# A decoder layer on one core: a larger share of the first down part in units of seven products, with two weight sums made by an accumulating DMA

## The chip, the cores and the metric

The kernel runs on one core of one Trainium2 chip. The metric is the device time of one execution in microseconds. Five engines have instruction queues of their own that run in order: TensorE (PE; its weight loads are shown as PEld), VectorE (DVE), ScalarE (ACT), GpSimd (POOL) and SyncE (SP). SP issues most loads, POOL some; they wait for one another through semaphores.

## The reference

One layer of a hybrid decoder, 256 tokens, width 2048, all in float32. What matters here is its last third:

```python
def conv_ffn(h, w_up, conv_w, conv_b, w_down):
    a, b = jnp.split(h @ w_up, 2, axis=-1)
    ...
    return (jax.nn.gelu(c, approximate=True) * b) @ w_down

    h = rms_norm(x, norm_ffn_pre[l])
    y = conv_ffn(h, ffn_w_up[l], ffn_conv_w[l], ffn_conv_b[l], ffn_w_down[l])
    x = x + rms_norm(y, norm_ffn_post[l])
```

`w_up` is 2048 x 11264, `w_down` 5632 x 2048. `c` is a causal convolution of width 3 over `a`. Before it come the mixer's parts: one projection `w_in` (with two gate blocks), two attentions, their output projections `wo_a` and `wo_b`, and `w_out`.

## The kernel before

Each float32 operand is split into a high part, rounded for TensorE, and the low part that is left. A product of a 128-row block is three matmuls: high x high, high x low, low x high (`mm3`, lines 174 to 177; a moving tile has 512 columns). `convert` splits a loaded weight tile: ScalarE casts the high part (L143), VectorE subtracts it (L144). Split tiles live in a ring of five, plain rows arrive through `raw` tiles loaded by SP.

Tokens go in two blocks of 128. A pair of 128-row weight blocks (k = 2u and 2u + 1) times two token blocks and two column halves of 512 is eight products, so 24 matmuls: a plain unit (`plain`). In a unit of seven (`seven`) the same is done as in Strassen's scheme by seven products, 21 matmuls, from sums of the four weight quarters (`ta`, `tb`, on VectorE, L232 to L235) and sums of the four token quarters (`s_of(u)`, made earlier by `token_sums`). Its products go to four accumulators `c` and four accumulators `q`; at the end of a part the `q` are added into `d` in a fixed order, and `c` on top of that.

`pair_gemm` runs a string of units, "p" plain and "s" seven. It is used for the gate part (one pair of column blocks of `w_in`, "psppspsp") and for the first down part: the first 24 of 44 row blocks of `w_down`, in two halves of 1024 columns (tiles `cd0`/`qd0`, `cd1`/`qd1`), twelve units each:

```python
PAIR_ORDER = ("psppsppsppsp", "ppsppsppsppp")
```

The two rows of a unit of seven are loaded by POOL, whole (1024 columns): `even` and `odd`, into a tile of tag `gp` (one buffer, for the odd-numbered sevens: `rr1`, `rr3`, ...) or into two tiles of tags `fa` and `fb` (two buffers each: `rr2a`, `rr2b`, ...). The `f` tags are shared with the up part's outputs `f0_5`, `f1_5`.

Most of the kernel is not written in its final order: a scheduler places each engine's instructions after their program order and the free buffers. Work that need not be done at once is put in by steps: `at(t, f)` keeps f for the t-th tick, `tick()` runs what is due.

Of the kernel before, what the change touches and what calls it, by code (L numbers as in the profile page):

```python
# [41 lines left out]
def trunk_layer(ctx, tc, x, x_cols_in, conv_cols_in, g_mix_post, g_ffn_post, w_in, w_q, w_kv,  # L42
                sinks, rel, wo_a, wo_b, w_out, w_up, w_down, rope_tab, strip_sel, out):
    nc = tc.nc
    vec, act, pe, pool = nc.vector, nc.scalar, nc.tensor, nc.gpsimd
# [13 lines left out]
    def sb(pl, shape, name, dt=F32, tag=None, bufs=None):  # L59
        return pl.tile(shape, dt, name=name, tag=tag or name, **({"bufs": bufs} if bufs else {}))  # L60
# [41 lines left out]
    cnt = [0]  # L102
# [52 lines left out]
    now = [0]  # L155

    def at(t, *fs):
        steps[max(t, now[0])].extend(fs)

    def tick():  # L160
        for f in steps.pop(now[0], ()):
            f()
        now[0] += 1

    def drain():
        while steps:
            tick()
# [33 lines left out]
    def banks(kind, name):  # L201
        return [(pacc if kind == 0 else (pss, pst)[i // 2]).tile([P, 512], F32, name=f"{name}{i}", tag="acc" if kind == 0 else "st"[i // 2])
                for i in range(4)]

    def pair_gemm(name, w, k0, c0, order, act_of, s_of, kind, d, place, sums):

        c11, c12, c21, c22 = c = banks(kind, f"c{name}_")
        q, used = [], set()
        row = lambda k: w[(k0 + k) * P:(k0 + k + 1) * P, c0:c0 + 1024]
        half = lambda w_, i: tuple(x[:, i * 512:(i + 1) * 512] for x in w_)  # L210

        def mul(o, x, w_, last=False):
            mm3(o, *x, *w_, id(o) not in used, last)
            used.add(id(o))

        def plain(u, last):
            for k in (2 * u, 2 * u + 1):
                w_ = convert(raw_row(row(k)), 1024)
                for t in range(NT):
                    for j in range(2):  # L220
                        mul(c[2 * t + j], act_of(k, t), half(w_, j), last and k % 2 == 1)
                tick()

        def seven(u, last):
            s1, s2, s3, s4 = s_of(u)
            even, odd = place()
            pool.dma_start(even, row(2 * u))
            pool.dma_start(odd, row(2 * u + 1))
# [4 lines left out]
            vec.tensor_tensor(ta[:, hi_], odd[:, hi_], even[:, hi_], op=ALU.subtract)  # L233
# [12 lines left out]
            tick()  # L246
            w_ = convert(tb, 1024)
            mul(q6, s2, half(w_, 0), last)
            mul(c21, act_of(2 * u + 1, 1), half(w_, 1))
            tick()  # L250
            if last:
                act.copy(d[0], q1)
                vec.tensor_tensor(d[1], d[0], q6, op=ALU.add)
                vec.tensor_tensor(d[2], d[1], q7, op=ALU.add)
                vec.tensor_tensor(d[3], d[2], q5, op=ALU.add)
                vec.tensor_tensor(d[1], d[1], q5, op=ALU.add)
# [11 lines left out]
    def token_sums(g, a, m, hi, lo):  # L268
# [4 lines left out]
        vec.tensor_tensor(m1, a21, a22, op=ALU.add)  # L273
        vec.tensor_tensor(m3, a11, a21, op=ALU.subtract)
        vec.tensor_tensor(m2, m1, a11, op=ALU.subtract)
# [82 lines left out]
    rh = sb(base, [P, NT], "rh")  # L358
# [297 lines left out]
    acc, _ = gemm(XH, XL, w_in, 0, KT, 0, 512)  # L656
# [4 lines left out]
    acc, _ = gemm(XH, XL, w_in, 0, KT, C_KV, KVR + ROPE)  # L661
# [54 lines left out]
    def gate_pair(j):  # L716
        d = [stg(f"tb{j + i}_{t}") for t in range(NT) for i in range(2)]
        c = pair_gemm("g", w_in, 0, C_GB + 512 * j, GATE_ORDER, lambda k, t: (XH(k)[:, t * P:(t + 1) * P], XL(k)[:, t * P:(t + 1) * P]),
                      lambda u: xs[u], 0, d, g_place, lambda: [sb(pg, [P, 1024], f"gt{n}{cnt[0]}", tag="gt" + n, bufs=2) for n in "ab"])
        for i, (o, x_) in enumerate(zip(d, c)):  # L720
            t = i // 2
            vec.tensor_tensor(o, o, x_, op=ALU.add)
            act.activation(o, o, AF.Tanh, scale=rh[:, t:t + 1])
        return [d[0], d[2]], [d[1], d[3]]

    tb = {0: gate_b(0)}
# [174 lines left out]
    es3, p3 = open_pool("p3")  # L901
# [5 lines left out]
    es6, p6 = open_pool("p6")  # L907
# [96 lines left out]
    for b in range(4):  # L1004
        c0, n = W_BLOCKS[b]
        last = b == 3
# [103 lines left out]
    gtiles, s_pool, s_of = [], [], {}  # L1110
# [10 lines left out]
    s_tiles = []  # L1121

    def g_sums(u):

        if u % 2 == 0:
            s_tiles.append(sb(p3, [P, D], f"s_{u // 2}", F32R, tag=f"x2_{u // 2}"))
        hi, lo = (s_tiles[u // 2][:, (u % 2) * 1024 + i * 512:(u % 2) * 1024 + (i + 1) * 512] for i in range(2))
        a, m = (sb(s_pool[0], [P, 512], f"s{n}{u}", tag="hx", bufs=2) for n in "am")
        s_of[u] = token_sums(gtiles[u].bitcast(F32), a, m, hi, lo)

    def gemm_cols(acc, c0):

# [40 lines left out]
    for c in range(1, 6):  # L1173
        if c == 2:
            for i in range(8):
                at(now[0] + i, lambda i=i: park(i // 4, i % 4))
        if c == 4:
            for u in range(4):
                at(now[0] + 3 + 3 * u, lambda u=u: g_sums(u))
        ffn_up(c, 4 * c)  # L1180

# [7 lines left out]
    def down_place():  # L1189
        sevens_done[0] += 1  # L1190
        i = sevens_done[0]
        if i % 2:
            both = sb(p6, [P, D], f"rr{i}", tag="gp")
            return both[:, 0:1024], both[:, 1024:2048]
        return [sb(p6, [P, 1024], f"rr{i}{n}", tag="f" + n, bufs=2) for n in "ab"]

    def f_sums():
        return [sb(p6, [P, 1024], f"t{n}{cnt[0]}", tag="f" + n, bufs=2) for n in "ab"]

    for p in range(2):  # L1200
        d = [dsum[t][2 * p + j] for t in range(NT) for j in range(2)]
        c = pair_gemm(f"d{p}", w_down, 0, 1024 * p, PAIR_ORDER[p], lambda k, t: (GH(k)[:, t * P:(t + 1) * P], GL(k)[:, t * P:(t + 1) * P]),
                      lambda u: s_of[u], p, d, down_place, f_sums)
        for o, x_ in zip(d, c):
            vec.tensor_tensor(o, o, x_, op=ALU.add)
# [44 lines left out]
    for j in range(4):  # L1250
        last = j == 3
# [103 lines left out]
```

## Time and profile before

| | |
|---|---|
| median of three runs | 1470.02 us (1469.75 to 1470.31) |
| profiled execution | 1469.86 us |
| its span, first to last instruction | 1468.0 us |
| TensorE busy | 1457.9 us, 7585 matmuls in the records |
| VectorE, ScalarE, GpSimd busy | 1044.5, 824.1, 61.7 us |
| first down part | 1002.35 to about 1128.3 us |

The page's idle time is what an engine spends without an instruction; only that of the engine on the chain costs time. A row of a group reads: line, engine, operation, output and inputs, shape, count, then busy time and mean. A POOL row of a DMA shows how long the issue took; the landing is told apart.

### The profile page before, as it was taken

To read this page: it belongs to the slowest core of one execution; us is meant where nothing else is said; L and a number is where in the kernel's file an instruction comes from. 1 tells how busy PE (TensorE), PEld (TensorE's weight loads), DVE (VectorE), ACT (ScalarE), POOL (GpSimd) and SP (SyncE) were. 2 spreads that over 40 slices of the span, in tenths; PEclk is the share of its full clock that TensorE was granted. 3 is DMA by queue.
4 is the path that set the end of the run, shared out by engine and by line. 5 is a ranking of instruction groups with operands and counts; after the bars stand their busy time and mean duration, and the time that the engine had idled before them with its cause. 6 is when DMAs were issued, how large, how long until landed. Compare 5 with 4: busy or idle time off the path is not lost.

```text
span 1468.0 us, 20901 instructions
## 1 busy us (share of the span) xinstructions
PE 1457.9 (99%) x7585; PEld 1246.1 (85%) x7585; DVE 1044.5 (71%) x1837; ACT 824.1 (56%) x1362; POOL 61.7 (4%) x107
## 2 busy tenths in 40 slices
PE   9999999999999999999999999999999999999997
PEld 7888888888888888888888888888888888888886
DVE  7788896646667665655699877678776676677556
ACT  7588874544565554444566655555454555555443
POOL 0022110000000010000000000000000000000000
PEclk9999999999999999999999999999999999999999
DMA  8755376466655559656665665655657656655653
GB/s 293 220 173 165 95 272 195 157 208 200 187 160 156 172 165 334 226 182 211 225 204 182 193 192 182 196 187 191 215 178 259 206 183 192 188 186 188 199 188 127
DMA packets 152467, 287.60 MB, mean 196 GB/s; under 512 B 18427, under 2 KB 29596, under 8 KB 152236
## 3 DMA queue, kind: packets, MB, share of 16 engines
q1 hardware_dynamic: 144736, 259.95, 55.2%
q0 software_dynamic: 7536, 26.27, 5.6%
q8 instruction: 59, 0.97, 0.3%
q14 instruction: 44, 0.36, 0.1%
q10 hardware_dynamic: 92, 0.05, 0.0%
HBM read 277.79 MB, written 8.44 MB: 195 GB/s over the span
## 4 chain that ended last, share of the span: by engine, by line
PE 97%; DVE 2%; ACT 1%; issue 0%; DMA 0%; DVEq 0%; ACTq 0%
PE accg L175 14%; PE accg L177 14%; PE accg L176 14%; PE ub L1138 10%; PE ua L1138 10%; PE ub L1142 5%; PE ua L1142 5%; PE cd L177 2%; PE cd L176 2%; PE cd L175 2%; PE mpo L866 1%; PE cg L175 1%; PE cg L177 1%; PE cg L176 1%; PE ms L832 1%; PE pt L521 1%
## 5 line engine op out<-in xcount | busy, mean ns | idle before, releaser
L144 DVE TENSOR_TENSOR wlo<-raw,whi 128x1024 fp32r<-128x1024 f32 (+2 forms) x482 | 583.8, 1215 | 313.2 <-ACT whi L143 306.5
L143 ACT CAST whi<-raw 128x1024 fp32r<-128x1024 f32 (+2 forms) x482 | 501.1, 1043 | 445.1 <-PE accg L177 212.8
L175 PE MATMUL accg<-whi,ahl 128*128 128x512 f32 (+1 forms) x480 | 187.9, 391 | 0.0
L177 PE MATMUL accg<-whi,ahl 128*128 128x512 f32 (+1 forms) x480 | 185.6, 387 | 0.0
L176 PE MATMUL accg<-wlo,ahl 128*128 128x512 f32 (+1 forms) x480 | 184.8, 385 | 0.0
L175 PE MATMUL accg<-whi,bhl 128*128 128x512 f32 x442 | 173.1, 392 | 0.0
L177 PE MATMUL accg<-whi,bhl 128*128 128x512 f32 x442 | 172.3, 390 | 0.0
L176 PE MATMUL accg<-wlo,bhl 128*128 128x512 f32 x442 | 172.2, 390 | 0.0
L1138 PE MATMUL ua<-ahl,whi 128*128 128x512 f32 x640 | 154.6, 391 | 0.0
L1138 PE MATMUL ub<-ahl,whi 128*128 128x512 f32 x640 | 154.6, 391 | 0.0
L1138 PEld LDWEIGHTS ub<-ahl,whi 128*128 128x128 f32 x640 | 117.5, 188 | 22.8 <-ACT cc L1036 0.2
L1138 PEld LDWEIGHTS ua<-ahl,whi 128*128 128x128 f32 x640 | 117.5, 188 | 22.7
L177 PEld LDWEIGHTS accg<-whi,ahl 128*128 128x128 f32 x480 | 90.1, 188 | 18.0
L176 PEld LDWEIGHTS accg<-wlo,ahl 128*128 128x128 f32 x480 | 90.3, 188 | 15.5
L175 PEld LDWEIGHTS accg<-whi,ahl 128*128 128x128 f32 x480 | 90.3, 188 | 15.4
L177 PEld LDWEIGHTS accg<-whi,bhl 128*128 128x128 f32 x442 | 83.0, 188 | 17.3
L176 PEld LDWEIGHTS accg<-wlo,bhl 128*128 128x128 f32 x442 | 83.0, 188 | 16.9
L175 PEld LDWEIGHTS accg<-whi,bhl 128*128 128x128 f32 x442 | 83.0, 188 | 16.9
L1142 PEld LDWEIGHTS ub<-ahl,wlo 128*128 128x128 f32 x640 | 82.2, 191 | 3.2
L1142 PEld LDWEIGHTS ua<-ahl,wlo 128*128 128x128 f32 x640 | 82.2, 191 | 3.1
L1142 PE MATMUL ua<-ahl,wlo 128*128 128x256 f32 x640 | 83.7, 283 | 0.0
L1142 PE MATMUL ub<-ahl,wlo 128*128 128x256 f32 x640 | 83.2, 283 | 0.0
(493 smaller groups left out, 2060.1 us busy)
## 6 DMA issues: line engine op xcount, KB each, us to landing
raw<-in_ffn_w_up_dram SPq DMA_DIRECT2D x176, 512.0 KB, 4.4
raw<-in_w_in_dram SPq DMA_DIRECT2D x105, 512.0 KB, 4.5
raw<-in_ffn_w_down_dram SPq DMA_DIRECT2D x74, 512.0 KB, 3.8
raw<-in_w_o_swa_dram SPq DMA_DIRECT2D x32, 512.0 KB, 4.3
raw<-in_w_o_mla_dram SPq DMA_DIRECT2D x32, 512.0 KB, 4.4
raw<-in_w_out_dram SPq DMA_DIRECT2D x32, 512.0 KB, 4.0
bias<-strip POOLq DMA_DIRECT2D x16, 256.0 KB, 4.3
raw<-in_mla_w_q_up_dram SPq DMA_DIRECT2D x32, 128.0 KB, 2.5
```

What stands on the lines that cost most here:

```text
L143: act.copy(hi[:, a:b], raw[:, a:b])
L144: vec.tensor_tensor(lo[:, a:b], raw[:, a:b], hi[:, a:b].bitcast(F32), op=ALU.subtract)
L175: pe.matmul(o, ah, bh, start=start, stop=False)
L176: pe.matmul(o, ah, bl, start=False, stop=False)
L177: pe.matmul(o, al, bh, start=False, stop=stop)
L521: pe.transpose(pt[:, j * P:(j + 1) * P], p[:, c * P:(c + 1) * P], ident)
L832: pe.matmul(o, w, v_, start=n == 0, stop=False)
L866: pe.matmul(o, w(t), p_[:, c], start=n == 0, stop=n == 5)
L1138: pe.matmul(acc[i], hi[:, c], hn[p][:, j * 512:(j + 1) * 512], start=p + j == 0, stop=stop)
L1142: pe.matmul(acc[i][:, 0:256], lo[:, c], hn[p][:, j * 512:j * 512 + 256], start=False, stop=False)
```

## The change

A second kind of unit of seven, `seven_dma`, is used in the first down part. POOL loads the even row into `x_`, the odd row into `odd`, the even row's left half once more into `even`, and then, with an accumulating DMA, adds the right halves of both rows onto `x_`. So `x_` holds even-left + even-right and even-right + odd-right, two of the four weight sums, with no instruction of VectorE; the other two (`y_`) are two additions. The signs of the token sums (`plus=True`) and of the closing sums are turned to match. The accumulating DMA waits on POOL's queue until the first load of `x_` has landed. The strings of units become "pspspspsppsp" and "ppspspspspsp": ten sevens in place of seven. The token sums of a fifth unit (`g_sums(4)`) are made in the up part, in a `gp` tile and two `hx` tiles. The closing sums of all pair parts, the gate part's too, are put in by steps (`first_sums`, `more_sums`, `finish_gate`) in place of at once, and the `drain()` after the gate part is gone.

```diff
+        def seven_dma(u, last):
+            s1, s2, s3, s4 = s_of(u)
+            x_, odd, y_, even = place()
+            lo_, hi_ = slice(0, 512), slice(512, 1024)
+            two = w[(k0 + 2 * u) * P:(k0 + 2 * u + 2) * P, c0 + 512:c0 + 1024].rearrange("(a p) n -> p a n", p=P)
+            pool.dma_start(x_, row(2 * u))
+            pool.dma_start(odd, row(2 * u + 1))
+            pool.dma_start(even[:, lo_], row(2 * u)[:, lo_])
+            pool.dma_start(x_.rearrange("p (a n) -> p a n", a=2), two, accum_op=ALU.add)
+            w_ = convert(odd, 1024)
...
+            mul(c11, act_of(2 * u + 1, 0), half(w_, 0))
+            mul(c12, s4, half(w_, 1))
+            w_ = convert(even, 512)
+            mul(q1, act_of(2 * u, 0), half(w_, 0), last)
+            w_ = convert(x_, 1024)
+            vec.tensor_tensor(y_[:, lo_], x_[:, lo_], odd[:, hi_], op=ALU.add)
+            vec.tensor_tensor(y_[:, hi_], y_[:, lo_], odd[:, lo_], op=ALU.add)
+            mul(q5, s1, half(w_, 0), last)
+            mul(q7, s3, half(w_, 1), last)
+            tick()
+            w_ = convert(y_, 1024)
+            mul(q6, s2, half(w_, 0), last)
+            mul(c21, act_of(2 * u + 1, 1), half(w_, 1))
+            tick()
...
+                at(now[0], first_sums)
+                at(now[0] + 1, more_sums)
...
-                seven(u, u == n - 1)
+                (seven if sums else seven_dma)(u, u == n - 1)
...
+        if plus:
+            vec.tensor_tensor(m1, a22, a21, op=ALU.subtract)
+        else:
+            vec.tensor_tensor(m1, a21, a22, op=ALU.add)
...
+        for n_, i in enumerate((0, 2, 1, 3)):
+            at(now[0] + n_, lambda i=i: finish_gate(i))
...
-    drain()
...
+        if u == 4:
+            t4 = sb(p6, [P, D], "s_tmp", tag="gp")
+            a, m = t4[:, 0:512], t4[:, 512:1024]
+            hi, lo = (sb(s_pool[0], [P, 512], f"s4{n}", F32R, tag="hx", bufs=2) for n in "hl")
...
+        f = lambda n: [sb(p6, [P, 1024], f"{n}{x_}{i}", tag="f" + x_, bufs=2) for x_ in "ab"]
         if i % 2:
             both = sb(p6, [P, D], f"rr{i}", tag="gp")
-            return both[:, 0:1024], both[:, 1024:2048]
+            x_, odd = both[:, 0:1024], both[:, 1024:2048]
+        else:
+            x_, odd = f("rr")
+        return x_, odd, *f("ty")
...
-PAIR_ORDER = ("psppsppsppsp", "ppsppsppsppp")
+PAIR_ORDER = ("pspspspsppsp", "ppspspspspsp")
```

The order of the instructions of POOL in the first half, before: the rows of the first four sevens (`rr1` to `rr4`; L227 loads an even row, L228 an odd one), with the storing of the residual between them.

```order
L227 DMA rr1_10019<-in_ffn_w_down_dram 128x1024
L228 DMA rr1_10019<-in_ffn_w_down_dram 128x1024
L1113 DMA x2_d_2541<-x2_1_5852 128x512 x4
L227 DMA rr2a_10180<-in_ffn_w_down_dram 128x1024
L227 DMA rr3_10299<-in_ffn_w_down_dram 128x1024
L228 DMA rr3_10299<-in_ffn_w_down_dram 128x1024
L228 DMA rr2b_10181<-in_ffn_w_down_dram 128x1024
L227 DMA rr4a_10417<-in_ffn_w_down_dram 128x1024
L228 DMA rr4b_10418<-in_ffn_w_down_dram 128x1024
```

In the changed kernel the same place, from the first seven on, reads as follows; L232 is the accumulating load (128x2x512), L231 the half tile `even` (`tyb`), L229 and L230 are x and odd.

```order
L229 DMA rra2_10141<-in_ffn_w_down_dram 128x1024
L232 DMA rra2_10141<-in_ffn_w_down_dram 128x2x512
L231 DMA tyb1_10031<-in_ffn_w_down_dram 128x512
L230 DMA rrb2_10142<-in_ffn_w_down_dram 128x1024
L229 DMA rr3_10237<-in_ffn_w_down_dram 128x1024
L230 DMA rr3_10237<-in_ffn_w_down_dram 128x1024
L232 DMA rr3_10237<-in_ffn_w_down_dram 128x2x512
L231 DMA tyb2_10144<-in_ffn_w_down_dram 128x512
L231 DMA tyb3_10239<-in_ffn_w_down_dram 128x512
L230 DMA rrb4_10320<-in_ffn_w_down_dram 128x1024
L231 DMA tyb4_10322<-in_ffn_w_down_dram 128x512
L229 DMA rra4_10319<-in_ffn_w_down_dram 128x1024
```

Each seven has four entries, and `tyb1` stands behind the accumulating load of the second seven, `tyb2` behind that of the third. `tyb2` takes the buffer of `rrb2`, the odd row of the same unit, and waits for the last reader of that; `rrb4` and `tyb4` take those of `tyb2` and `tyb3`, and wait until these are split. `rra4`, the fourth unit's x, stands behind `tyb4`.

On VectorE, before, around the first sums of the second seven (`ta682`, `tb682` from `rr2a`, `rr2b`; `wlo` is the low part of a split, `raw` a plain row):

```order
L232 TENSOR_TENSOR ta682_10184<-rr2a_10180 128x512
L1041 TENSOR_TENSOR uu23_10168<-uu23_10168,cc23_10167 128x256
L310 TENSOR_TENSOR ghl10_7551<-uu21_10070,ghl10_7551 128x256
L144 TENSOR_TENSOR wlo675_10085<-raw674_10082,whi675_10084 128x1024
L144 TENSOR_TENSOR wlo677_10103<-raw676_10100,whi677_10102 128x1024
L310 TENSOR_TENSOR ghl11_7552<-uu22_10119,ghl11_7552 128x256
L144 TENSOR_TENSOR wlo679_10134<-raw678_10131,whi679_10133 128x1024
L1043 SCALAR_TENSOR_TENSOR uu23_10168<-uu23_10168,cc23_10167 128x256
L233 TENSOR_TENSOR ta682_10184<-rr2b_10181,rr2a_10180 128x512
```

In the changed kernel, at the same place (the two plain rows behind the first seven, then the second seven; `tya2` is its y):

```order
L144 TENSOR_TENSOR wlo675_10095<-raw674_10092,whi675_10094 128x1024
L144 TENSOR_TENSOR wlo677_10113<-raw676_10110,whi677_10112 128x1024
L144 TENSOR_TENSOR wlo678_10150<-rrb2_10142,whi678_10149 128x1024
L242 TENSOR_TENSOR tya2_10143<-rra2_10141,rrb2_10142 128x512
L1094 TENSOR_SCALAR uu23_10189<-uu23_10189 128x256
L243 TENSOR_TENSOR tya2_10143<-tya2_10143,rrb2_10142 128x512
L1095 TENSOR_TENSOR uu23_10189<-uu23_10189,cc23_10188 128x256
L1097 SCALAR_TENSOR_TENSOR uu23_10189<-uu23_10189,cc23_10188 128x256
L1098 TENSOR_TENSOR uu23_10189<-uu23_10189,f1_5_9967 128x256
L363 TENSOR_TENSOR ghl11_7552<-uu23_10189,ghl11_7552 128x256
L144 TENSOR_TENSOR wlo679_10160<-tyb2_10144,whi679_10159 128x512
L144 TENSOR_TENSOR wlo680_10167<-rra2_10141,whi680_10166 128x1024
```

The second seven now comes behind one plain unit where it had two, its odd row is split as the third wide tile after the first seven, and its half tile `tyb2` is split right after the two sums and the last steps of the convolution.

More of the change, by code (lines that the diff above doesn't have):

```diff
@@ L222, in plain, with first_sums, more_sums @@
                 tick()
+        def seven_dma(u, last):
[8 more added lines that the diff above has]
+            w_ = convert(odd, 1024)
+            if not q:
+                q[:] = banks(1 - kind, f"q{name}_")
+            q1, q5, q7, q6 = q
+            mul(c11, act_of(2 * u + 1, 0), half(w_, 0))
[12 more added lines that the diff above has]
+            tick()
+            if last:
+                d0, d1, d2, d3 = d() if callable(d) else d
+                def first_sums():
+                    act.copy(d0, q1)
+                    vec.tensor_tensor(d1, d0, q6, op=ALU.subtract)
+                    vec.tensor_tensor(d2, d1, q7, op=ALU.add)
+                def more_sums():
+                    vec.tensor_tensor(d3, d2, q5, op=ALU.add)
+                    vec.tensor_tensor(d1, d1, q5, op=ALU.add)
+                at(now[0], first_sums)
+                at(now[0] + 1, more_sums)
         def seven(u, last):
@@ L251, in seven, with first_sums, more_sums @@
             if last:
[L252 to L256, printed above, removed]
+                d0, d1, d2, d3 = d() if callable(d) else d
+                def first_sums():
+                    act.copy(d0, q1)
+                    vec.tensor_tensor(d1, d0, q6, op=ALU.add)
+                    vec.tensor_tensor(d2, d1, q7, op=ALU.add)
+                def more_sums():
+                    vec.tensor_tensor(d3, d2, q5, op=ALU.add)
+                    vec.tensor_tensor(d1, d1, q5, op=ALU.add)
+                at(now[0], first_sums)
+                at(now[0] + 1, more_sums)
         n = order.count("s")
@@ L266, in pair_gemm, with token_sums @@
         return c
-    def token_sums(g, a, m, hi, lo):
+    def token_sums(g, a, m, hi, lo, plus=False):
         vec.tensor_tensor(a, g[:, 0:512], g[:, 512:1024], op=ALU.add)
@@ L272, in token_sums @@
         m1, m2, m3, m4 = (m[:, i * P:(i + 1) * P] for i in range(4))
-        vec.tensor_tensor(m1, a21, a22, op=ALU.add)
+        if plus:
+            vec.tensor_tensor(m1, a22, a21, op=ALU.subtract)
+        else:
+            vec.tensor_tensor(m1, a21, a22, op=ALU.add)
         vec.tensor_tensor(m3, a11, a21, op=ALU.subtract)
-        vec.tensor_tensor(m2, m1, a11, op=ALU.subtract)
+        vec.tensor_tensor(m2, m1, a11, op=ALU.add if plus else ALU.subtract)
         vec.tensor_tensor(m4, a12, m2, op=ALU.subtract)
@@ L719, in gate_pair, with finish_gate @@
                       lambda u: xs[u], 0, d, g_place, lambda: [sb(pg, [P, 1024], f"gt{n}{cnt[0]}", tag="gt" + n, bufs=2) for n in "ab"])
[L720 to L723, printed above, removed]
+        def finish_gate(i):
+            vec.tensor_tensor(d[i], d[i], c[i], op=ALU.add)
+            act.activation(d[i], d[i], AF.Tanh, scale=rh[:, i // 2:i // 2 + 1])
+        for n_, i in enumerate((0, 2, 1, 3)):
+            at(now[0] + n_, lambda i=i: finish_gate(i))
         return [d[0], d[2]], [d[1], d[3]]
@@ L1123, in g_sums @@
     def g_sums(u):
[L1125 to L1129, printed above, removed]
+        if u == 4:
[3 more added lines that the diff above has]
+        else:
+            if u % 2 == 0:
+                s_tiles.append(sb(p3, [P, D], f"s_{u // 2}", F32R, tag=f"x2_{u // 2}"))
+            hi, lo = (s_tiles[u // 2][:, (u % 2) * 1024 + i * 512:(u % 2) * 1024 + (i + 1) * 512] for i in range(2))
+            a, m = (sb(s_pool[0], [P, 512], f"s{n}{u}", tag="hx", bufs=2) for n in "am")
+        s_of[u] = token_sums(gtiles[u].bitcast(F32), a, m, hi, lo, True)
     def gemm_cols(acc, c0):
@@ L1177, in trunk_layer @@
         if c == 4:
-            for u in range(4):
+            for u in range(5):
                 at(now[0] + 3 + 3 * u, lambda u=u: g_sums(u))
@@ L1191, in down_place @@
         i = sevens_done[0]
+        f = lambda n: [sb(p6, [P, 1024], f"{n}{x_}{i}", tag="f" + x_, bufs=2) for x_ in "ab"]
         if i % 2:
             both = sb(p6, [P, D], f"rr{i}", tag="gp")
-            return both[:, 0:1024], both[:, 1024:2048]
-        return [sb(p6, [P, 1024], f"rr{i}{n}", tag="f" + n, bufs=2) for n in "ab"]
-    def f_sums():
-        return [sb(p6, [P, 1024], f"t{n}{cnt[0]}", tag="f" + n, bufs=2) for n in "ab"]
+            x_, odd = both[:, 0:1024], both[:, 1024:2048]
+        else:
+            x_, odd = f("rr")
+        return x_, odd, *f("ty")
     for p in range(2):
@@ L1202, in trunk_layer @@
         c = pair_gemm(f"d{p}", w_down, 0, 1024 * p, PAIR_ORDER[p], lambda k, t: (GH(k)[:, t * P:(t + 1) * P], GL(k)[:, t * P:(t + 1) * P]),
-                      lambda u: s_of[u], p, d, down_place, f_sums)
-        for o, x_ in zip(d, c):
-            vec.tensor_tensor(o, o, x_, op=ALU.add)
+                      lambda u: s_of[u], p, d, down_place, None)
+        for n_, (o, x_) in enumerate(zip(d, c)):
+            at(now[0] + n_, lambda o=o, x_=x_, n_=n_: vec.tensor_tensor(o, x_, o, op=ALU.subtract if n_ % 2 else ALU.add))
     gpost2 = sb(p6, [P, D], "gpost2", tag="gp")
```

## The prediction

> **What bounds the kernel now.** I read the page's first lines and its chain first, then the waits of TensorE, then stretches of the down part. The page:
>
> ```profile
> span 1468.0 us, 20901 instructions
> ...
> PE 1457.9 (99%) x7585; PEld 1246.1 (85%) x7585; DVE 1044.5 (71%) x1837; ACT 824.1 (56%) x1362; POOL 61.7 (4%) x107
> ...
> PE 97%; DVE 2%; ACT 1%; issue 0%; DMA 0%; DVEq 0%; ACTq 0%
> ```
>
> TensorE is busy for 99% of the span and 97% of the chain that ends last is TensorE. All that it waited for in the whole run:
>
> ```profile
> PE warm L77 <- DVE ramp L66: 1.1, 1, 1.1
> PE pstrip L341 <- DMA sel<-in_strip_sel_dram: 0.3, 1, 0.3
> ```
>
> Both lie in the first microseconds. So time can only go with matmuls, and come only with waits that do not exist yet. The stretches view (columns: stretch, length, then busy time and count of PE, PEld, DVE, ACT, POOL, granted clock, DMA share, GB/s) shows the first down part's first plain unit, its first seven-product unit, the whole part, a stage of `wo_a`, and the gate part:
>
> ```profile
> 1002.35:1007.81 5.46, 5.46 (x26) 4.52 (x25) 5.17 (x10) 3.44 (x7) 1.06 (x2) 1.00 0.24 74
> 1007.81:1012.59 4.78, 4.78 (x23) 3.96 (x22) 4.78 (x10) 3.88 (x6) 0.53 (x1) 1.00 0.79 276
> 1002.35:1128.30 125.95, 125.95 (x557) 104.31 (x556) 97.96 (x114) 63.46 (x72) 6.33 (x12) 1.00 0.63 212
> 547.00:583.70 36.70, 36.70 (x167) 30.36 (x167) 18.91 (x20) 15.89 (x17) 5.32 (x11) 1.00 0.93 330
> 235.00:300.00 65.00, 65.00 (x287) 53.55 (x286) 42.92 (x45) 33.24 (x36) 2.17 (x4) 1.00 0.53 174
> ```
>
> A plain unit takes TensorE 5.46 us, a unit of seven 4.78 us, and the 125.95 us of the part hold no idle time.
>
> **The change part by part.** *Three more units of seven.* Each takes the place of a plain one: 3 x (5.46 - 4.78) = 2.04 us less. That is all there is to win.
>
> *The arithmetic around it.* Weight sums on VectorE fall from 7 x 4 to 10 x 2, eight fewer; but a unit of seven splits 3.5 tiles where a plain one splits 2, so three more units split 4.5 tiles more. With the rows below (0.68 us a sum, 1.21 us a tile) that is -5.4 and +5.4 us: VectorE stays at 97.96 of 125.95 us. The fifth unit's token sums lie in the up part. In the gate part no matmul moves and TensorE is full there, with VectorE at 42.92 of 65.00 us: the later closing sums cost nothing as long as that spare time hides them. If it did not, their 2.7 us would be late. At the seam of the two halves the four closing sums (2.75 us) and one split between them (1.22 us) must end before the second matmul group of the next half: they have the last plain unit's 5.46 us and so about 2 us to spare, and the last seven of the second half, which now has one plain unit behind it, has the same.
>
> *The loads.* GpSimd's queue issues 40 loads for these units where it issued 14, and each accumulating one waits on that queue until the load under it has landed; what is queued behind it waits too. The rows of that queue today, and of landings (size, median us to landing):
>
> ```profile
> 992.71 0.54 POOL L227 DMA_DIRECT2D rr2a<-in_ffn_w_down_dram  x1 [249.18 <-ACT whi L143]
> 1005.20 0.54 POOL L227 DMA_DIRECT2D rr<-in_ffn_w_down_dram  x1 [11.95 <-DVE ghl L310]
> 1005.73 0.53 POOL L228 DMA_DIRECT2D rr<-in_ffn_w_down_dram  x1
> ```
>
> ```profile
> rr<-in_ffn_w_down_dram POOLq DMA_DIRECT2D x6, 512.0 KB, 5.2
> gpost<-in_norm_ffn_post_dram POOLq DMA_DIRECT2D x1, 1024.0 KB, 8.3
> ...
> rr4a<-in_ffn_w_down_dram POOLq DMA_DIRECT2D x1, 512.0 KB, 3.7
> ```
>
> The two loads at 1005.20 and 1005.73, asked for one by one, landed after 3.8 and 4.7 us, so 1.4 us apart:
>
> ```profile
> rr<-in_ffn_w_down_dram POOLq DMA_DIRECT2D x1, 512.0 KB, 3.8
> ```
>
> ```profile
> rr<-in_ffn_w_down_dram POOLq DMA_DIRECT2D x1, 512.0 KB, 4.7
> ```
>
> No row has an accumulating transfer; call its time from issue to landing A. It is not shorter than the fastest plain load of its size, 3.7 us; it touches 512 KB twice, so 1 MB, and the 1 MB load took 8.3 us. I take 5.2 us: 3.8 for a load and 1.4 for the second pass, also the median load of the queue.
>
> [...]
>
> *Where the loads come late: the second unit.* Its first product starts at 1007.81 + 4.78 + 5.46 = 1018.05. In the order shown above, its half tile `tyb2` takes the place of its own odd row, so it is loaded only after VectorE has split that row and made both sums from it. Today's third 1024-wide split after the first seven, which stands where the odd row's now does, and a sum:
>
> ```profile
> 1004.89 1.22 DVE L144 TENSOR_TENSOR wlo<-ta,whi 128x1024 fp32r<-128x1024 f32 x1
> ...
> 1008.22 0.33 DVE L1040 TENSOR_SCALAR uu<-uu 128x256 f32<-128x256 f32 x1
> ...
> 1012.34 1.21 DVE L144 TENSOR_TENSOR wlo<-raw,whi 128x1024 fp32r<-128x1024 f32 x1
> 1013.48 0.41 DVE L1043 SCALAR_TENSOR_TENSOR uu<-uu,cc 128x256 f32<-128x256 f32 x1
> 1013.81 0.68 DVE L233 TENSOR_TENSOR ta<-rr2b,rr2a 128x512 f32<-128x512 f32 x1
> ```
>
> 1012.34 + 1.21 + two sums of 0.68 + one small operation of 0.33 gives 1015.2. Loads of 256 KB on that queue took:
>
> ```profile
> DMA to landing us min/median/max: 2.9/3.9/5.7
> ```
>
> (the merge stage's `lta`). So `tyb2` lands at 1019.1. Then come, in order, its own high part, the high part of x (rows below) and the low part of x (1.22):
>
> ```profile
> 1017.25 0.61 ACT L143 CAST whi<-rr2a 128x512 fp32r<-128x512 f32 x1
> 1017.96 1.06 ACT L143 CAST whi<-ta 128x1024 fp32r<-128x1024 f32 x1
> ```
>
> 0.61 + 1.06 + 1.22 = 2.89, ready at 1022.0. A matmul of the unit takes 4.78 / 21 = 0.23 us, and TensorE wants it after 9 of the 21 and one more: 1018.05 + 2.05 + 0.23 = 1020.3. The wait is 1.7 us; with 2.9 and 5.7 us for the landing, 0.7 and 3.5. Later units reload from tiles of the unit before, and have this time to spare.
>
> *The fourth unit.* The load issued at 992.71 (tile `rr2a`) landed after
>
> ```profile
> DMA to landing us min/median/max: 4.4/4.4/4.4
> ```
>
> us. The fourth unit's x is queued on GpSimd behind `tyb4`, which waits for the third unit's half tile to be split. After 1022.0 VectorE still has four splits of 1.22 and a half one: 1027.5. One issue of 0.54 later x goes out, lands after 4.4 at 1032.5, and the sum lands at 1032.5 + A = 1037.7. The unit starts at 1018.05 + 1.7 + 2 x 10.24 = 1040.2; y must be ready 15 matmuls and one more later, at 1043.9, and before it stand three sums and two splits, 4.5 us. So the sum may land at 1039.4: 1.7 us to spare, and nothing lost while A is under 6.9.
>
> In the second half the loads of a unit go out a whole pair of units (20 us) ahead, and 4.4 + A fits.
>
> *Sum.* -2.04 + 1.7 = -0.3 us. The profiled execution took 1469.86 us, 1.86 us more than its span, and lies 0.16 us under the median; against the median, 1470.02 - 0.3 = **1469.7 us**. With the ends: -2.04 + 0.7 gives 1468.7; A = 8.3 gives 1472.2 (next part). About 0.2%, 2.9 us, is what a measurement of this kernel can tell from no change, so this is no change.
>
> **The rivals.** *The accumulating load is slow.* From A = 7.2 on, the third unit's sum (issued when its x has landed: split of the first x until about 1006.8, and 4.4, so 1011.2) is still in the queue when `tyb2` is asked for at 1015.2, and `tyb2` lands 0.7 us (half of 1.4) behind it: each us of A is then lost at the second unit, and another at the fourth, whose loads are started later by it. The waits are 2.0 + 2 x (A - 7.2). For A = 8.3 that is 4.2, so 2.2 us slower; at A = 8.7 it becomes slower by more than 2.9 us; at 10.4, twice a median load, 8.4 - 2.0 = 6.4 us slower: 1476.4 us. For it: nobody has measured A here, and loads of the queue reached 8.3 us. Against: that one was 1 MB from DRAM. [...]
>
> *Everything is in time.* If the landings of the second unit are early or its splits are, the whole 2.04 us stay: 1468.0 us. Against it stand the rows above: even 2.9 us is 0.7 too late.
>
> *The DMA engines become the bound.* A pair of a plain unit and a seven loads 1.05 + 1.84 = 2.9 MB, and 3.4 MB with what the addition reads back, in 10.24 us: 333 GB/s, where the seven's stretch now has 276. If 276 were all, a pair would take 12.4 us, and ten pairs 21 us more: 1491 us. Against: 330 GB/s flowed from 547 us on with TensorE full.
>
> *It does not do what it says.* The order has ten units with ten accumulating loads and nine matmuls fewer; it does.
>
> **How the numbers follow.** Forecast 0.55, all in time 0.12, slow accumulating load 0.26, DMA bound 0.05, and 0.02 for a gain elsewhere that I do not see. The first two are within 0.2%, so same is 0.67; slower 0.31; faster 0.02, since 2.04 us is under the bound. The range goes from 1468.0 (all in time) to 1477.0, the slow load's price and a little; beyond it lie the DMA bound and an A over 11, about 0.15 together.
>
> **What would show it.** In the changed kernel's waits of TensorE there should be one in the down part, of 1 to 2 us near 1020, put down to VectorE's or ScalarE's split of x of the second unit, with `tyb2` landing near 1019; the accumulating loads should land 5 to 6 us after issue; the part should hold 14 x 5.46 + 10 x 4.78 us of matmuls. Two waits, at the second and the fourth unit, with A over 7, mean the first rival. No wait at all, and 2 us gained, mean the second. Waits of ScalarE for plain rows through the whole part mean the third. Waits in the second half or at a seam would make the working wrong.

## The result, and the profile after

The changed kernel takes **1487.93 us** (median of four runs, 1487.42 to 1489.23) against 1469.88 us before (1469.54 to 1470.31): 1.0122 times as long, with a 95% interval of 1.011 to 1.0134. Forecast were 1469.7 us, in a range of 1468.0 to 1477.0. The profiled execution took 1489.23 us.

The page's first lines of the changed kernel, and its chain by engine:

```profile
span 1487.4 us, 20957 instructions
...
PE 1463.7 (98%) x7576; PEld 1247.4 (84%) x7576; DVE 1045.5 (70%) x1841; ACT 828.9 (56%) x1369; POOL 82.9 (6%) x133
...
PE 24%; DMA 3%; issue 2%; DVE 2%; POOL 0%; ACT 0%; DVEq 0%; ACTq 0%; POOLq 0%
```

Nine matmuls are gone (7585 to 7576) as the change says, yet TensorE is busy 5.8 us longer: the same matmuls run slower somewhere. The waits of TensorE (line, what ended the wait, us in total, times, longest):

```profile
PE qd L176 <- DVE wlo L144: 5.5, 2, 3.5
PE qd L175 <- ACT whi L143: 4.5, 1, 4.5
PE cd L176 <- DVE wlo L144: 1.9, 1, 1.9
PE cd L175 <- DVE ds L261: 1.6, 1, 1.6
```

Five waits, 13.5 us, where there was none. In the trace they begin at 1019.8 us (second unit of seven, 4.5 us), 1050.6 (fourth, 2.0), 1076.2 (the seam of the halves, 1.6), 1112.7 (eighth, 3.5) and 1129.7 (the plain unit behind the ninth, 1.9); the expectations below call the last two the ninth and the tenth unit, after the transfers that VectorE stood before. The stretches view of some of these places (columns as before; PE's busy time first, the granted clock third from the end):

```profile
1019.00:1024.70 5.70, 1.24 (x7) 0.70 (x5) 0.05 (x1) 0.70 (x2) 0.00 (x0) 0.98 0.67 171
1024.70:1032.00 7.30, 7.30 (x17) 5.15 (x18) 7.01 (x7) 5.51 (x7) 0.53 (x1) 0.55 0.48 135
1116.60:1120.20 3.60, 3.57 (x9) 2.84 (x10) 3.60 (x4) 1.04 (x1) 0.53 (x1) 0.53 0.58 211
```

Behind the two long waits the clock stands at about half: 17 matmuls take 7.30 us where 17 x 0.23 = 3.9 would do (3.4 us lost, some of it short waits for splits), and 9 take 3.6 in place of 2.1 (1.5 us).

The sum over the whole part: I took each step of TensorE from one matmul's start to the next between 990 and 1150 us, less the 0.228 us of a full-speed step. Steps that are over 0.05 us longer than that add up to an excess of 20.5 us; the kernel before has none. 14.2 us of it lie in the five waits, the other 6.2 in slower steps, most of them at half clock, where a step took 0.43 us. -2.04 for the matmuls, +20.5, and 0.7 us by which the part begins later (1003.05 against 1002.35 us) make 19.1 us; the spans differ by 1487.4 - 1468.0 = 19.4.

Now the accumulating transfer itself. The view of its line (issue time in ns, minimum, median, maximum; who waited for it; landing):

```profile
L232 POOL DMA_DIRECT2D rr<-in_ffn_w_down_dram x5: 1191/1204/1227, 889.4 to 1103.6; - x5
...
  DVE tya L242: 15.1, 4
...
DMA to landing us min/median/max: 6.5/8.0/10.9
```

It lands after 8.0 us, not 5.2, and its issue takes 1.2 us, not 0.53. VectorE stood 15.1 us before its sum `tya` for it, in the four places where the profile names the transfer. What stood behind that sum is seen in VectorE's timeline at the fourth, the eighth and the plain unit behind the ninth (start, length, line, output and inputs, in brackets the idle time ahead and what ended it):

```profile
1051.11 0.69 DVE L242 TENSOR_TENSOR tya<-rr 128x512 f32<-128x512 f32 x1 [4.15 <-issue]
1051.71 1.22 DVE L144 TENSOR_TENSOR wlo<-tya,whi 128x1024 fp32r<-128x1024 f32 x1
...
1114.02 0.69 DVE L242 TENSOR_TENSOR tya<-rr 128x512 f32<-128x512 f32 x1 [6.10 <-DMA rr<-in_ffn_w_down_dram]
...
1115.35 1.22 DVE L144 TENSOR_TENSOR wlo<-tya,whi 128x1024 fp32r<-128x1024 f32 x1
...
1129.35 0.69 DVE L242 TENSOR_TENSOR tya<-rra,rrb 128x512 f32<-128x512 f32 x1 [4.62 <-DMA rra<-in_ffn_w_down_dram]
...
1130.68 2.35 DVE L144 TENSOR_TENSOR wlo<-raw,whi 128x1024 fp32r<-128x1024 f32 x2
```

Read the names in VectorE's order: the sum at 1051.11 is that of the *fifth* unit (`rr`, so an odd one), and the split behind it is the last of the *fourth*, for which TensorE waited from 1050.6 on (the row names no releaser; the fifth unit's transfer landed at 1051.03). At 1114.02 it is the ninth unit's sum, with the eighth unit's last split behind it; at 1129.35 the tenth unit's, with the two rows of the plain unit behind the ninth. The idle engine had work that was ready, behind an instruction that was not: for the fourth unit's last split, ScalarE's part began at 1045.93 us and took 1.06 us.

At the second unit it is the half tile, in GpSimd's timeline and on the chain of waits:

```profile
1009.42 0.53 POOL L229 DMA_DIRECT2D rr<-in_ffn_w_down_dram  x1 [0.95 <-DVE wlo L144]
...
1015.81 1.21 POOL L232 DMA_DIRECT2D rr<-in_ffn_w_down_dram  x1 [5.34 <-DVE tya L243]
1016.54 1.76 POOL L231 DMA_DIRECT2D tyb<-in_ffn_w_down_dram  x2
```

```profile
1016.54 7.36 DMA tyb<-in_ffn_w_down_dram
```

`tyb2` was asked for 0.73 us behind the third unit's accumulating load and landed after 7.36 us; the accumulating load landed at 1023.25 us, the half tile at 1023.90. The accumulating load itself went out late: the third unit's x, the first row, was asked for at 1009.42 us, when the first unit's x had been split, and landed 6.1 us later, at 1015.52.

### The profile page after: what moved, and what is told of

Read it like the earlier page. It is cut to its first block, busy times and chain, and to the rows that moved or that the text cites. A ratio compares the mean times of both kernels' runs of the same rounds, so it can differ in the third digit from the quotient of the medians.

```text
span 1487.4 us, 20957 instructions
## 1 busy us (share of the span) xinstructions
PE 1463.7 (98%) x7576; PEld 1247.4 (84%) x7576; DVE 1045.5 (70%) x1841; ACT 828.9 (56%) x1369; POOL 82.9 (6%) x133
## 2 busy tenths in 40 slices
DMA packets 155988, 295.47 MB, mean 199 GB/s; under 512 B 18747, under 2 KB 29916, under 8 KB 155756
## 5 line engine op out<-in xcount | busy, mean ns | idle before, releaser
L144 DVE TENSOR_TENSOR wlo<-raw,whi 128x1024 fp32r<-128x1024 f32 (+2 forms) x476 | 576.1, 1214 | 301.3 <-ACT whi L143 294.1
L143 ACT CAST whi<-raw 128x1024 fp32r<-128x1024 f32 (+2 forms) x476 | 494.8, 1043 | 434.0 <-PE accg L177 203.7
```

The lines of the kernel that those rows point to most:

```text
L143: act.copy(hi[:, a:b], raw[:, a:b])
L144: vec.tensor_tensor(lo[:, a:b], raw[:, a:b], hi[:, a:b].bitcast(F32), op=ALU.subtract)
```

## The experiments

**Theory:** the accumulating transfer lands later than taken, and what stands behind it waits: on GpSimd's queue, on VectorE, or both. **Rivals:** the traffic of the DMA engines; the string of ten sevens and its buffers, whoever makes the sums; GpSimd's queue alone. In each group of runs the median of the kernel before lay between 1469.99 and 1470.36 us.

**1. The same transfer, without the addition.**

```diff
-            pool.dma_start(x_.rearrange("p (a n) -> p a n", a=2), two, accum_op=ALU.add)
+            pool.dma_start(x_.rearrange("p (a n) -> p a n", a=2), two)
```

> The transfer of the right halves is a plain load over x instead of an accumulating one, same shape, same queue, same order; the addition (two weight sums) is left out. Theory (the accumulating transfer is slow to land, 6.5 to 10.9 us, and holds what stands behind it on GpSimd's queue): the same transfer lands in 4 to 5 us, its issue falls from 1.2 to about 0.55 us, most of the five waits go, time 1468 to 1473 us. Rival (traffic: the DMA engines are 0.9 busy in the part, and it is the bytes that count): the landings stay near 7 us and the time stays at 1485 to 1489 us, since the load moves as many descriptors and hardly fewer bytes.

Measured: 1476.58 us, 1.0041 of the kernel before (1.0026 to 1.0056), so 11.4 us less than the changed kernel. The view of the line and the longest waits:

```profile
L232 POOL DMA_DIRECT2D rr<-in_ffn_w_down_dram x5: 717/717/728, 888.7 to 1094.7; - x5
...
DMA to landing us min/median/max: 4.6/6.3/8.3
```

```profile
PE cd L176 <- DVE wlo L144: 2.8, 1, 2.8
PE qd L175 <- ACT whi L143: 1.3, 1, 1.3
```

Between the two: the bytes alone are not it, but a plain load in this place also takes 6.3 us. The addition costs 1.7 us of landing (8.0 - 6.3) and 0.5 us of issue, and the kernel 11.4 us. Traffic as the only cause is out; my expectation of 4 to 5 us to landing and at most 1473 us was too low.

**2. Ten sevens with all sums on VectorE.** The kernel before with the new string, and the token sums of a fifth unit.

```diff
-PAIR_ORDER = ("psppsppsppsp", "ppsppsppsppp")
+PAIR_ORDER = ("pspspspsppsp", "ppspspspspsp")
```

> The kernel before with the new string of units alone: ten sevens, all four weight sums of each on VectorE, no accumulating transfer. Theory (only the accumulating transfer and the queue behind it cost): a gain of up to 2.04 us, unless VectorE, which then has about 9.5 of 10.24 us filled per pair of units, comes late: 1468 to 1472 us. Rival (ten sevens in such a string do not fit, whoever sums): waits at the second, fourth, ninth and tenth unit, 1480 to 1488 us.

Measured: 1469.87 us, ratio 0.9999 (0.9989 to 1.0008), one wait of 0.8 us at the second unit. Ten sevens as such cost nothing; the rival of the string falls.

**3. Accumulating transfers in the old string.** The changed kernel with the seven sevens of the kernel before.

```diff
-PAIR_ORDER = ("pspspspsppsp", "ppspspspspsp")
+PAIR_ORDER = ("psppsppsppsp", "ppsppsppsppp")
```

> The changed kernel with the old string of units: seven sevens by accumulating transfers, mostly with two plain units between. Theory: a transfer of about 8 us fits into 15.7 us per unit and two plain ones; no wait over 3.4 us, 1469 to 1473 us. Rival (the late closing sums, the signs and the gate part cost, or each accumulating transfer costs by itself, 17.9/10 us each): 1480 to 1484 us.

Measured: 1472.89 us, ratio 1.0018 (1.0009 to 1.0028). The transfers land after 9.4 us (median), and there is one wait of over 0.2 us:

```profile
PE qd L175 <- ACT whi L143: 2.3, 1, 2.3
```

```profile
1026.50:1031.00 4.50, 4.27 (x12) 3.18 (x13) 4.50 (x5) 3.68 (x4) 1.08 (x2) 0.68 0.45 137
```

The second row is the stretch behind the wait, with the clock at 0.68. So a transfer of 8 to 10 us is not dear in itself; in the changed kernel it is dear where sevens follow each other with one plain unit between. This kernel has the later closing sums and the turned signs too, and its wait and the slow steps behind it (together 4.7 us of excess) cover the 3.8 us by which its span is longer: those edits cost nothing that shows.

**4. Two of the loads on another queue.** The odd row and the half tile are issued by SyncE.

```diff
-            pool.dma_start(odd, row(2 * u + 1))
-            pool.dma_start(even[:, lo_], row(2 * u)[:, lo_])
+            nc.sync.dma_start(odd, row(2 * u + 1))
+            nc.sync.dma_start(even[:, lo_], row(2 * u)[:, lo_])
```

> The changed kernel with the odd row and the half tile loaded by SyncE's queue; GpSimd keeps x and the accumulating transfer. Theory (small loads stuck behind the accumulating transfer on GpSimd's queue): the half tiles land in 3 to 4 us, the waits at the second and ninth unit go, 1470 to 1477 us. Rival (only the accumulating transfer's own length counts, or the traffic): the waits at the fourth and tenth unit and the seam stay or grow, 1483 to 1489 us, or plain rows on SyncE's queue come late in their place.

Measured: 1484.54 us, ratio 1.0092 (1.0075 to 1.0109): 3.4 us of 18 come back. The half tile of the second unit no longer waits behind a transfer, but the accumulating ones land after 8.5 us and VectorE stands before them as before:

```profile
  DVE tya L242: 14.6, 3
```

```profile
PE qd L176 <- DVE wlo L144: 6.8, 4, 3.1
PE cd L176 <- DVE wlo L144: 4.8, 2, 3.1
```

GpSimd's queue is a small part of it.

**5. A buffer of its own for the second unit's half tile.**

```diff
+        if i == 2:
+            return x_, odd, sb(p6, [P, 1024], "tya2", tag="fa", bufs=2), sb(p6, [P, 512], "ty_own", tag="jk", bufs=1)
         return x_, odd, *f("ty")
```

> The changed kernel with a buffer of its own for the second unit's half tile, so that it is loaded long before and stands first on GpSimd's queue. Theory (the wait at the second unit is the reload of tyb2 behind the third unit's accumulating transfer; with its clock loss it costs about 8 us): the wait of 4.6 us at 1019.8 us and the half clock from 1024.5 to 1031.3 us go, 1478 to 1482 us; the waits of the second half stay. Rival (x or y of the second unit is as late as its half tile, or the later units only wait longer instead): 1485 to 1488 us.

Measured: 1488.58 us, ratio 1.013 (1.0114 to 1.0146), no gain. The late half tile is gone and the wait at 1020.9 us is as long (4.7 us), for another reason. VectorE's timeline there:

```profile
1023.32 0.69 DVE L242 TENSOR_TENSOR tya<-rr 128x512 f32<-128x512 f32 x1 [6.24 <-DMA rr<-in_ffn_w_down_dram]
1024.05 0.69 DVE L243 TENSOR_TENSOR tya<-tya,rr 128x512 f32<-128x512 f32 x1
1024.66 1.22 DVE L144 TENSOR_TENSOR wlo<-tya,whi 128x1024 fp32r<-128x1024 f32 x1
```

With the earlier half tile the scheduler set the third unit's sums ahead of the second unit's last split, and VectorE stood 6.24 us before the third unit's transfer. My theory of the second unit was half a cause: the pattern that took its place is that of the rows of the changed kernel above.

**6. No third transfer at all.** The line of the accumulating load is left out.

> The changed kernel without the third 512 KB transfer of a unit, neither accumulating nor plain (two weight sums are left out). Theory (what the plain load in its place still cost, 6.6 us over the kernel before, is the transfer's being there: bytes and place in the queue): 1467.5 to 1470 us, at most the wait at the second unit under 1 us. Rival (those 6.6 us come from the buffers and the closing sums, not from that transfer): 1474 to 1477 us again.

Measured: 1469.31 us, ratio 0.9994 (0.9985 to 1.0004), one wait of 0.5 us. The 18 us hang on that transfer, for without it the sum has nothing late to wait for; buffers and closing sums keep about 1 us at most (experiment 8 below, with as many matmuls, takes 1468.49 us).

**7. Work put into the wait.**

```diff
             mul(c12, s4, half(w_, 1))
+            if sevens_done[0] == 2:
+                for _ in range(5):
+                    mul(c12, s4, half(w_, 1))
```

> The changed kernel with one product of the second unit made six times, 15 matmuls of 0.23 us (3.4 us) more work on TensorE just ahead of its 4.6 us wait (one accumulator comes out otherwise). Theory (the wait takes the clock down, and the half clock behind it costs some 3 us): the work lies in the wait, no half clock behind 1024 us, time 3 us shorter than the changed kernel, 1484 to 1486 us. Rival (the low clock in the records costs nothing that the matmuls' pace shows, or it has another cause): 1487.5 to 1491 us.

Measured: 1491.67 us, ratio 1.0145 (1.0129 to 1.0162). The 4.5 us wait shrank to 1.0, but the 3.4 us of extra matmuls moved every later unit, and new waits and half clocks stand at other places. Behind a wait of 3.7 us at 1049.9 us:

```profile
1054.00:1060.00 6.00, 6.00 (x16) 4.63 (x16) 4.18 (x4) 1.04 (x1) 1.46 (x2) 0.53 0.78 199
```

Inconclusive as a test of what half the clock costs; that cost is read from the stretches only.

**8. Ten sevens on VectorE in another string.** As in experiment 2, but two plain units between the first two sevens.

```diff
-PAIR_ORDER = ("pspspspsppsp", "ppspspspspsp")
+PAIR_ORDER = ("psppspspspsp", "ppspspspspsp")
```

> Ten sevens with all sums on VectorE as in the second experiment, but with two plain units between the first two sevens of the first half (s at places 1, 4, 6, 8 and 10), which gives the one unit that waited there 5.5 us more. Theory (that wait of 0.8 us and the small losses around it ate the gain of 2.04 us): no wait over 0.3 us, span 1466 us, 1468.0 us, ratio 0.9986. Rival (the string only moves the wait to the next pair of units, since VectorE has 9.5 of 10.24 us filled): 1469 to 1471 us.

Measured: 1468.49 us, ratio 0.9987 (0.9978 to 0.9996): the 2.04 us of nine fewer matmuls, nearly whole. No wait in the part, and VectorE filled for 88% of it:

```profile
1000.00:1126.20 126.20, 126.20 (x560) 104.58 (x559) 111.44 (x135) 69.65 (x80) 9.49 (x18) 1.00 0.64 209
```

This is the one version whose interval against the kernel before lies wholly below 1, if only by 0.13% (1.85 us between the medians), and it needs no accumulating transfer.

**New theory:** what costs is VectorE's order. It has the next unit's sum ahead of a split that TensorE wants now, and that is harmless only while the transfer lands early. **Rival:** each unit waits for its own late transfer, whatever the order.

**9. The same work and transfers, other buffers.** y and the half tile take turns in `fa`, so y of unit n+1 needs the buffer of y of unit n, and its sum cannot stand ahead of that unit's last split.

```diff
-        f = lambda n: [sb(p6, [P, 1024], f"{n}{x_}{i}", tag="f" + x_, bufs=2) for x_ in "ab"]
+        f = lambda n, tag: [sb(p6, [P, 1024], f"{n}{x_}{i}", tag=tag, bufs=2) for x_ in "ab"]
...
-            x_, odd = f("rr")
-        return x_, odd, *f("ty")
+            x_, odd = f("rr", "fb") if i > 2 else (None, None)
+        if i == 2:
+            x_ = sb(p6, [P, 1024], "rra2", tag="fb", bufs=2)
+            y_, odd = f("ty", "fa")
+            return x_, odd, y_, sb(p6, [P, 512], "ty_own", tag="jk", bufs=1)
+        return x_, odd, *f("ty", "fa")
```

> The changed kernel with its tiles in other buffers, the same work and the same transfers: y and the half tile in the fa buffers, x and odd of the even-numbered sevens in fb (the second unit's half tile in a buffer of its own, its odd row in fa). Then the sum of unit n+1 needs the buffer of y of unit n, and VectorE's order has it behind that unit's last split, no longer ahead of it. Theory (TensorE waits since VectorE stands before a sum of the next unit, whose accumulating transfer has not landed, with a split that is wanted now queued behind it): the waits at 1019.8, 1050.6 and 1112.7 us and the half clock behind them go, the transfers still take about 8 us; 1470 to 1476 us. Rival (each unit waits for its own accumulating transfer or half tile, whatever VectorE's order): 1484 to 1490 us.

Measured: 1476.85 us, ratio 1.0042 (1.0027 to 1.0057): 11.1 us less than the changed kernel, while the transfers land *later* than there. The waits, the landing, and what is left in VectorE's timeline:

```profile
PE cd L176 <- DVE wlo L144: 5.6, 3, 2.4
```

```profile
DMA to landing us min/median/max: 6.8/10.0/11.2
```

```profile
1038.49 1.23 DVE L144 TENSOR_TENSOR wlo<-tya,whi 128x1024 fp32r<-128x1024 f32 x1
1044.87 0.69 DVE L242 TENSOR_TENSOR tya<-rr 128x512 f32<-128x512 f32 x1 [5.15 <-DMA rr<-in_ffn_w_down_dram]
...
1046.21 2.35 DVE L144 TENSOR_TENSOR wlo<-raw,whi 128x1024 fp32r<-128x1024 f32 x2
```

The sum now stands behind the split of `tya`, as meant, and still ahead of the splits of two plain rows. All three waits left are for such rows. The other buffers move the loads as well: the fourth unit's accumulating load goes out 19.6 us ahead of TensorE's first matmul with that unit's x, where it was 11.5 in the changed kernel. So this run by itself doesn't part the order from the earlier start; experiment 11 does.

**10. That, with the string of experiment 8.** Only the string differs.

> The same with the string that gained in the kernel with VectorE's sums (first half: s at places 1, 4, 6, 8 and 10). Theory: what is left at the second unit goes too, 1468 to 1473 us; the transfers still take about 8 us, so a wait remains where a plain unit's split stands behind a sum. Rival (the transfers are the bound): no faster than the run before it, 1484 to 1490 us.

Measured: 1475.49 us, ratio 1.0036 (1.0024 to 1.0049). The intervals of this run and the one before overlap; the expected 1473 us was not reached. Waits for plain rows are left, and one of 2.3 us at the seam.

**11. The sums behind the plain rows too.** One VectorE instruction per plain unit ahead of a seven (eight in all), one element wide, ties the last y to that unit's last split.

```diff
+                if tie and len(last_y) > 1 and k % 2:
+                    vec.tensor_tensor(sb(p6, [P, 512], f"tie_{name}{u}", tag="jk", bufs=1)[:, 0:1], last_y[-1][:, 0:1], w_[1][:, 0:1].bitcast(F32), op=ALU.add)
```

> The run before it with one element-wide instruction of VectorE behind the last split of each plain unit ahead of a seven (from the third seven on), which reads the last y and that split, so that VectorE's order has the sums of a unit behind the plain unit's splits as well. The transfers and their order stay nearly as they were. Theory (what is left, 8 us over a part without waits, is a sum of the next unit standing ahead of plain splits): the waits put down to a split of a plain row go, 1468 to 1471 us, with accumulating transfers still at 8 to 10 us. Rival (a late accumulating transfer is only moved to the unit itself: its sum and the split behind it are then late): 1474 to 1480 us, with waits put down to splits of x or y.

Measured: 1468.92 us, ratio 0.9997 (0.9988 to 1.0006). The one wait left in the part, the view of the accumulating transfers (the sum is line 247 here), and VectorE at the fifth unit's sum, now behind the splits of the two plain rows and with no idle time before it:

```profile
PE cd L175 <- DVE ds L266: 0.7, 1, 0.7
```

```profile
  DVE tya L247: 1.1, 1
...
DMA to landing us min/median/max: 6.0/8.4/11.3
```

```profile
1045.68 2.35 DVE L144 TENSOR_TENSOR wlo<-raw,whi 128x1024 fp32r<-128x1024 f32 x2
...
1049.76 0.68 DVE L247 TENSOR_TENSOR tya<-rr 128x512 f32<-128x512 f32 x1
```

The same ten transfers, as slow as in the changed kernel (8.4 us against 8.0), and VectorE waits 1.1 us for them in place of 15.1. 19 us are back. About 6 of them, from experiment 10 to this one, come from VectorE's order alone; the other 13 from buffers and the string of units, which set that order but also when loads can start. The earlier start is not what removed the waits of the second half: the ninth and tenth accumulating loads landed 13.1 and 10.1 us ahead of TensorE's first matmul with their own x in the changed kernel, and land 7.8 and 8.5 us ahead here. They come later for their own unit, and nothing waits. The theory is shown for the splits behind a sum; the rival, that the unit itself would then be late, is not borne out.

## Why the prediction was wrong

- *Three more sevens win 2.04 us:* right. Experiment 8 has a span of 1466.4 us, 1.6 under the kernel before, and a median 1.85 us lower.
- *VectorE's work stays level, the closing sums of the gate part and the signs cost nothing:* right. VectorE is busy 1045.5 us (1044.5 before), and experiment 6 has all those edits at 1469.31 us, within 1 us of experiment 8, which has neither the signs nor the later closing sums.
- *An accumulating load takes A = 5.2 us and 0.53 us of issue:* mis-sized. 8.0 us (6.5 to 10.9) and 1.2 us. Of the 2.8 us missing, 1.1 belong to the plain load of this size in this place too (6.3 in experiment 1), 1.7 to the addition: 8.0 against 6.3 is 1.27 times. That the first rival's 10.4 us, twice a median load, is what such a load takes, no run shows: the medians of landing are 7.9 to 10.0 us.
- *The second unit waits 1.7 us, `tyb2` lands near 1019:* 4.5 us and 1023.9. It was asked for at 1016.54, not 1015.2, and took 7.36 us, not 3.9, since it stood right behind the third unit's accumulating load and landed 0.65 us behind that. This is the first rival's mechanism (it had 0.7), but not from the cause that it named, a large A: this load landed after 7.44 us, for which the rival's formula gives 2.5 us of waits in all. It went out at 1015.81 us, not at 1011.2. The first unit's x was split until 1009.13, not 1006.8, so the third unit's x was asked for that much later, and it took 6.1 us, not 4.4. Both terms grew against those that the prediction had used.
- *The fourth unit has 1.7 us to spare; in the second half a pair of units ahead fits:* this is the step that failed. I worked out when a unit's own sum is needed, and by that rule it held: the fourth unit's own sum began at 1044.40 and its last split could have begun at 1047.0, 4 us before TensorE stood waiting for it. In the second half every accumulating load landed 10.1 us or more ahead of TensorE's first matmul with its own x. I did not ask what stands behind that sum on VectorE, nor where the *next* unit's sum stands. From the fifth unit on it stands ahead of a split of the present unit or of the plain unit, so the transfer must land by that split's time, a unit or two earlier than its own unit needs it: TensorE wanted the eighth unit's last split from 1113.1 us on, and VectorE made it behind the sum of the ninth unit's transfer, which landed at 1113.83, while TensorE's first matmul with the ninth unit's x came at 1126.97. Three of the five waits come from this, and experiments 9 and 11 undo them. I showed VectorE's order at the second unit alone; there, and at the third and fourth, the sum stands behind its own unit's first split, and so late enough.
- *Two us to spare at the seam:* wrong by the same cause, one step removed. The chain of waits there:

```profile
1058.43 8.09 DMA rra<-in_ffn_w_down_dram
...
1066.64 0.70 DVE tya L242
...
1067.98 1.23 DVE wlo L144
...
1069.22 5.25 DMA raw<-in_ffn_w_down_dram
...
1074.57 1.06 ACT whi L143
1075.66 1.23 DVE wlo L144
1076.88 0.60 DVE ds L260
1077.48 0.61 DVE ds L261
...
1078.13 0.50 PE cd L175
```

  The sixth unit's transfer holds its sum, that holds the split of a plain row, that row's buffer is reloaded late (5.25 us), and the last closing sum stands behind the split of the row so loaded.
- *The first rival's price, 2.0 + 2 x (A - 7.2):* at the measured 8.0 us it gives 3.6 us of waits, 1.6 us slower. The direction was right and the size wrong by a factor of ten, since it too counted own due times at two units only, and had no term for a lower clock, which stood at 0.55 and 0.53 in the stretches behind the two long waits.
- *The DMA engines as the bound:* no. Experiment 11 moves the same bytes in a part without waits over 1 us. The records count 295.47 MB for the changed kernel and for experiment 1 alike, so what the addition reads back shows in neither.

That the prediction's last paragraph named "waits in the second half or at a seam" as what would make its working wrong was true: three of the five lie there.

## What to carry to other kernels

Ask of each new wait on an in-order engine not only when its own consumer needs it, but what the engine has queued behind it and when that is needed: the earlier of the two is its due time. When an asynchronous producer is slower than a scheduler assumed, look at the order before the transfer: here other buffers, another string and a few one-element instructions brought back 19 us with the transfer as slow as ever. And before moving work to a slow path, see whether the engine it leaves was full: VectorE at 88% made all ten units' sums in time.

## What the runs showed of the hardware

- An accumulating DMA of 512 KB took GpSimd 1.2 us per issue and landed after a median of 7.9 to 10.0 us (6.0 to 12.2 in all; the changed kernel and experiments 3, 4, 5, 9, 10 and 11); the plain one of the same shape and place 0.72 us and 6.3 us. In the changed kernel the half tiles (256 KB) asked for 0.7 us behind one landed 0.6 to 0.7 us after it, four times out of four.
- The clock fell behind some waits and not behind others. It stood at 0.55 and 0.53 in the stretches behind the changed kernel's waits of 4.5 and 3.5 us, at 0.68 behind one of 2.3 us (experiment 3), at 0.68 behind one of 1.3 us in experiment 1 (1020.80 to 1024.50 us), and at 0.57 behind one of 2.4 us in experiment 9:

```profile
1047.60:1051.50 3.90, 3.90 (x11) 3.08 (x12) 3.23 (x3) 0.00 (x0) 1.01 (x1) 0.57 0.68 132
```

  Behind the changed kernel's wait of 2.0 us at the fourth unit it stayed at 1.00, and behind experiment 1's of 2.8 us too:

```profile
1050.60:1056.00 5.40, 3.33 (x14) 2.10 (x13) 4.89 (x6) 1.27 (x2) 0.53 (x1) 1.00 0.45 147
```

```profile
1119.00:1124.00 5.00, 5.00 (x23) 4.12 (x24) 4.97 (x5) 1.06 (x1) 0.00 (x0) 1.00 0.74 220
```

  So the length of a wait alone does not decide, and what else does, these runs do not show. In the clock records of the changed kernel's first down part, half clock stands from 1024.51 to 1031.34 us and from 1116.67 to 1120.09 us, and full clock elsewhere. How much of the 18 us the half clock cost by itself stays open too.
